# A state-space layer kernel: step-size columns moved into the token-major projection, decay tiles on VectorE one step ahead, row transposes one step later

## The chip, the cores and the metric

The kernel runs on one core of one Trainium2 chip. The metric is device microseconds of the whole program, from first to last instruction of one execution. Before the change it took 2696.54 us (median of 3 runs, 2694.78 to 2699.78).

## The reference, cut to what matters

Two layers over 1024 tokens of width 1024. Each layer mixes tokens in three ways (differential attention, dilated attention, a Mamba-2 state-space scan with 6 heads in chunks of 128 tokens) and then applies a gated MLP.

```python
proj = h @ w_in[layer]                       # 1024 x 3206 columns
dq, dk, dv, lq, lk, lv, z, xbc, dt = jnp.split(proj, IN_OFFSETS, axis=-1)
...
dt = jax.nn.softplus(dt + dt_bias)           # 6 columns: the step sizes
a = dt * A                                   # per head and token
Lmat = jnp.exp(segsum(a))                    # decay inside a chunk
xdt = x * dt_c[..., None]
y_diag = einsum('bclgn,bcsgn->bcgls', Cm, Bm) * Lmat @ xdt      # inside a chunk
y_off = Cm @ prev * jnp.exp(a_cs)            # from the chunks before
y = (y_diag + y_off + x * D) * jax.nn.silu(z)
out = grouped_rms_norm(y) * norm_gain        # two groups of 192 columns
...
mix = concatenate([o_diff, o_dil, o_ssd]) @ w_out[layer]
x = x + rms_norm(mix, post_mix_norm[layer])
```

## The kernel before

Every layer works on the tokens in two halves (T = 0 and 1, 512 tokens each). All projections are float32 products made of three fp32r matmuls: activations and weights are split into a high and a low part, and high x high, high x low and low x high are added in PSUM. `wsplit` (L130 to L134) loads a weight tile of 128x1024 (tile `wr`, 3 buffers, its DMA issued on SP's queue), copies it to `wh` on ScalarE (L133) and subtracts on VectorE to get `wl` (L134); `wh` and `wl` have 4 buffers each.

Most projections have the weights stationary and 512 tokens moving (`mm3`, L202, L205, L206). The columns that are needed token-major (dilated V, differential V, the gate z) come from `tm_in` through `tm_units` (L152, L155, L156): here 128 tokens are stationary and weight columns move. A *unit* is one block of columns for one tile of 128 tokens, 24 matmuls. `tm_in` has two blocks of 512 columns; each block takes four weight tiles, two of the eight row groups each, and four units, one for each token tile. So the next block's first weight tile can be split only when the last unit of the block before has gone past the buffer, and its fourth tile can be loaded only when the first one's split has given a `wr` buffer back. The evacuation (L772 to L777) copies the columns out, applies the gate and stores them to DRAM tensor `VZ`.

The six step-size columns have their own path, `dt_unit(T)` (L425 to L466): 16 matmuls with 12 or 6 stationary columns and 512 moving tokens, 8 small selecting matmuls that turn the 12 rows into token-major columns (L436), a chain of small VectorE instructions on 128x24 tiles for softplus (L439 to L459), and four matmuls for the running sums (L464).

The scan is `ssd(T)` (L470 to L581), a generator with 14 steps for four chunks. The first step of a chunk loads its rows (`cxa` from CX, `cxz` from VZ), builds two decay tiles of 128x768 (L502: the high part on POOL, the low part on VectorE, tiles named P), transposes x (L506, `xdt`, L508 and L510), and multiplies the decay tiles by a triangle (L528, L529). The second step masks (L532), calls `finish` for the chunk before (L481 to L488: three transposes of its normalised rows `yq`, L483) and reads the carried state (L543). The third step is the product inside the chunk (L552), the new state (L558) and the grouped norm, which ends in two ScalarE copies that write `yq` (L575).

`weave(dense, mixer, counts)` sets the order: for each dense unit it lets `counts` steps of a mixer generator go in behind given matmuls of the unit. Three weaves follow each other in a layer: units of the second attention and the scan's inputs beside attention(0) and the two `dt_unit`s; units for half 1 and `tm_in(1)` beside the rest of attention(0) and ssd(0); and the first output units (`out_units(0)`) beside what is left. After the output units come the rest of `tm_in(1)`, with the normalisation of half 0 (`pre_a`, `pre_b`, `norm_add`, L236 to L270) in between (`follow`). Differential attention's output norm is deferred in two parts: `f1` (L665 to L677, a VectorE chain with one POOL instruction) and `f2` (four transposes, L682) two steps behind.

Of the kernel before, what the change touches and what calls it, by code (L numbers as in the profile page):

```python
# [19 lines left out]
NL = 2  # L20
# [43 lines left out]
K_ID, K_SEL, K_TRI, K_MD, K_ML = 0, 128, 148, 276, 276 + 640  # L64
# [5 lines left out]
def body(ctx, tc, x_in, win, wtm, wdt, wout, wup, wdn, cst, gains, dtb, alog, lamp, kst, rope, out):  # L70
# [15 lines left out]
    sel = kc[:, K_SEL:K_SEL + 8]  # L86
    mhalf = kc[:, K_SEL + 8:K_SEL + 16]
# [15 lines left out]
    def tiny(n=4):  # L103
        return ss.tile([P, 8], F32, tag="tiny", bufs=16, name="tiny")
# [23 lines left out]
    def wsplit(src, nk):  # L128
        raw = sp.tile([P, KT * P], F32, tag="wr", bufs=3, name="wr")
        Y.dma_start(raw[:, :nk * P].rearrange("p (a n) -> p a n", a=src.shape[1]) if len(src.shape) == 3 else raw[:, :nk * P], src)  # L130
        hi = sp.tile([P, KT * P], F32R, tag="wh", bufs=4, name="wh")
        lo = sp.tile([P, KT * P], F32R, tag="wl", bufs=4, name="wl")
        A.activation(hi[:, :nk * P], raw[:, :nk * P], AF.Copy)  # L133
        V.tensor_tensor(lo[:, :nk * P], raw[:, :nk * P], fr(hi[:, :nk * P]), op=ALU.subtract)  # L134
# [11 lines left out]
    def tm3(a, pair, tk, hi, lo, k0, nk, n0, n):  # L146
        for k in range(nk):
            kk = k0 + k
            w = slice(k * H, (k + 1) * H)
            xh, xl = pair[kk]  # L150
            xh, xl = xh[:, tk], xl[:, tk]
            i = T_.matmul(a[:], xh, hi[:, w], start=(n0 + k == 0), stop=False)  # L152
            if n0 + k == 0 and hold[0] is not None:
                queue_behind(i, hold[0])
            T_.matmul(a[:], xh, lo[:, w], start=False, stop=False)  # L155
            lastmm[0] = T_.matmul(a[:], xl, hi[:, w], start=False, stop=(n0 + k == n - 1))  # L156
        marks.append(lastmm[0])

    def tm_units(w, k0, nk, pair, evac, before=None, inner=False, pairs=0):

        def tiles(c):
            return [(i, min(2, nk - i)) + wsplit(w[c, :, k0 + i:k0 + min(i + 2, nk)], min(2, nk - i) * 4)
                    for i in range(0, nk, 2)]

        def unit(c, t, ts):
            a = acc()
            for i, n, hi, lo in ts:
                tm3(a, pair, slice(t * P, (t + 1) * P), hi, lo, i, n, i, nk)
            evac(c, t, a)

        if inner:
            ts = [tiles(c) for c in range(2)]
            for t in range(4):
                for c in range(2):
                    unit(c, t, ts[c])
                    yield
            return
        for c in range(2):
            ts = tiles(c)
            if c < pairs:  # L180
                for t in (0, 2):
                    aa = [acc(), acc()]
                    for i, n, hi, lo in ts:
                        for x in range(2):
                            tm3(aa[x], pair, slice((t + x) * P, (t + x + 1) * P), hi, lo, i, n, i, nk)
                        if i == 2:
# [109 lines left out]
    for l in range(NL):  # L296
        lam_init = 0.8 - 0.6 * math.exp(-0.3 * l)
        def layer_constants():
# [23 lines left out]
            wd = ss.tile([P, KT, 12], F32R, tag="wd", bufs=1, name="wd")  # L322
# [750 lines left out]
```

## Time and profile before

| | before |
|---|---|
| median of 3 runs | 2696.54 us (2694.78 to 2699.78) |
| the profiled execution, and its span | 2697.55 us, 2695.8 us |
| PE (TensorE matmul) busy | 2625.3 us, 97% |
| DVE (VectorE) busy | 1830.1 us, 68% |
| ACT (ScalarE) busy | 1246.8 us, 46% |
| POOL (GpSimd) busy | 252.4 us, 9% |

PE executes its instructions in order, and matmuls overlap: a 512-column matmul is drawn 0.39 us long but the next one starts 0.227 us later. So the cost of a matmul is read from start to start. An entry in brackets, such as `[2.11 <-POOL P L502]`, is idle time of that engine just before the instruction and what ended it. PEclk is the granted clock as a share of 2.4 GHz.

### The profile page before, as it was taken

The numbers are of one execution on the slowest core, as the hardware profiler recorded it, in microseconds if no ns is written. First come the engines' busy times: TensorE is split into PE (matmuls) and PEld (weight loads), VectorE is DVE, ScalarE is ACT, GpSimd is POOL, SyncE is SP. The second block draws the span as 40 slices with busy tenths as digits, with TensorE's granted clock in tenths as the row PEclk, the third lists the DMA queues.
The fourth block names the chain that finished last, engine by engine and source line by source line (L and its number), as shares of the span: only waits on it lengthen the run. The fifth ranks groups of instructions, "written<-read, shape, count | busy, mean of one in ns | idle before, by whom it ended". The sixth has DMA issues, their size and how long they took to land. (4 is left out here: it accounts for less than half of the span.)

```text
span 2695.8 us, 36379 instructions
## 1 busy us (share of the span) xinstructions
PE 2625.3 (97%) x13160; PEld 2135.6 (79%) x13160; DVE 1830.1 (68%) x3814; ACT 1246.8 (46%) x2167; POOL 252.4 (9%) x244
## 2 busy tenths in 40 slices
PE   7999999999999999999999999999999999999998
PEld 5887777888778877888888877778887888788886
DVE  5566767566877676666765677575678775956666
ACT  4463444555544444333444644455555344543333
POOL 0100220110002010000002002201100110100001
PEclk9999999999999999999999999999999999999999
DMA  6653546343333354233257536354344334633222
GB/s 226 215 175 111 187 150 186 108 129 114 99 123 124 117 185 156 94 97 99 85 182 228 160 107 204 118 187 114 106 125 134 99 117 125 229 97 101 94 95 70
DMA packets 157348, 368.82 MB, mean 137 GB/s; under 512 B 18032, under 2 KB 53744, under 8 KB 157168
## 3 DMA queue, kind: packets, MB, share of 16 engines
q1 hardware_dynamic: 157168, 366.49, 43.4%
q8 instruction: 104, 1.70, 0.3%
q14 instruction: 76, 0.62, 0.1%
HBM read 306.13 MB, written 60.29 MB: 136 GB/s over the span
## 5 line engine op out<-in xcount | busy, mean ns | idle before, releaser
L202 PE MATMUL acc<-ah,wh 128*128 128x512 f32 x1952 | 775.6, 398 | 0.5 <-ACT ah L253 0.5
L205 PE MATMUL acc<-al,wh 128*128 128x512 f32 x1952 | 764.5, 392 | 0.0
L206 PE MATMUL acc<-ah,wl 128*128 128x512 f32 x1952 | 763.6, 391 | 0.0
L134 DVE TENSOR_TENSOR wl<-wr,wh 128x1024 fp32r<-128x1024 f32 (+1 forms) x390 | 470.5, 1209 | 264.1 <-ACT wh L133 259.8
L133 ACT ACTIVATE wh<-wr 128x1024 fp32r<-128x1024 f32 (+1 forms) x390 | 403.9, 1040 | 432.9 <-PE acc L205 254.4
L202 PEld LDWEIGHTS acc<-ah,wh 128*128 128x128 f32 x1952 | 367.1, 188 | 81.6 <-issue 9.6
L206 PEld LDWEIGHTS acc<-ah,wl 128*128 128x128 f32 x1952 | 367.2, 188 | 77.5 <-issue 1.0
L205 PEld LDWEIGHTS acc<-al,wh 128*128 128x128 f32 x1952 | 367.5, 188 | 73.0 <-issue 1.2
L361 DVE SCALAR_TENSOR_TENSOR cv<-acc,cs,cv 128x511 f32<-128x511 f32 (+2 forms) x436 | 324.4, 744 | 12.2 <-ACT cv L359 10.3
L152 PE MATMUL acc<-wh,g 128*128 128x512 f32 x704 | 282.3, 401 | 7.7 <-DVE ustate L364 3.7
L155 PE MATMUL acc<-wl,g 128*128 128x512 f32 x704 | 277.2, 394 | 3.0 <-DVE wl L134 3.0
L156 PE MATMUL acc<-wh,g 128*128 128x512 f32 x704 | 275.1, 393 | 0.6 <-DVE g L820 0.6
L598 ACT ACTIVATE P<-P,tiny 128x128 f32<-128x128 f32 (+7 forms) x224 | 173.2, 774 | 146.8 <-DVE tiny L597 141.4
L595 DVE CUSTOM_DVE_ANT_0 P<-s,kc 128x512 f32<-128x512 f32 (+3 forms) x224 | 130.5, 588 | 122.2 <-PE s L593 115.8
L155 PE MATMUL acc<-wl,ah 128*128 128x512 f32 x512 | 204.8, 401 | 7.5 <-DVE wl L134 7.4
L152 PE MATMUL acc<-wh,ah 128*128 128x512 f32 x512 | 205.4, 404 | 4.3 <-ACT ah L253 2.4
L156 PE MATMUL acc<-wh,al 128*128 128x512 f32 x512 | 203.6, 400 | 2.8 <-DVE al L254 2.8
L115 POOL TENSOR_TENSOR rs_r<-rs_m,kc 128x1 f32<-128x1 f32 (+2 forms) x88 | 66.0, 754 | 1337.6 <-DVE rs L116 1326.8
L152 PEld LDWEIGHTS acc<-wh,g 128*128 128x128 f32 x704 | 132.9, 189 | 42.2 <-issue 7.1
L359 ACT ACTIVATE cv<-acc,cs 128x512 f32<-128x512 f32 x204 | 155.5, 762 | 9.2 <-PE acc L206 8.2
L840 DVE TENSOR_TENSOR fT<-acc,fT 128x512 f32<-128x512 f32 x160 | 108.7, 686 | 73.0 <-PE acc L156 72.5
L156 PEld LDWEIGHTS acc<-wh,g 128*128 128x128 f32 x704 | 132.7, 189 | 31.0 <-DVE g L820 3.4
(183 smaller groups left out, 3169.4 us busy)
## 6 DMA issues: line engine op xcount, KB each, us to landing
wr<-in_wup SPq DMA_DIRECT2D x176, 512.0 KB, 3.6
wr<-in_wdn SPq DMA_DIRECT2D x80, 512.0 KB, 3.6
wr<-in_win SPq DMA_DIRECT2D x54, 512.0 KB, 4.5
wr<-in_wtm SPq DMA_DIRECT2D x32, 512.0 KB, 5.3
wr<-in_wout SPq DMA_DIRECT2D x32, 512.0 KB, 4.3
xd<-t SPq DMA_DIRECT2D x24, 512.0 KB, 2.9
t<-xd SPq DMA_DIRECT2D x24, 512.0 KB, 3.7
t<-in_x SPq DMA_DIRECT2D x16, 512.0 KB, 4.8
```

The lines of the kernel that those rows point to most:

```text
L133: A.activation(hi[:, :nk * P], raw[:, :nk * P], AF.Copy)
L134: V.tensor_tensor(lo[:, :nk * P], raw[:, :nk * P], fr(hi[:, :nk * P]), op=ALU.subtract)
L152: i = T_.matmul(a[:], xh, hi[:, w], start=(n0 + k == 0), stop=False)
L155: T_.matmul(a[:], xh, lo[:, w], start=False, stop=False)
L156: lastmm[0] = T_.matmul(a[:], xl, hi[:, w], start=False, stop=(n0 + k == n - 1))
L202: i = T_.matmul(a[:], hi[:, w], xh, start=(k == 0), stop=False)
L205: T_.matmul(a[:], hi[:, w], xl, start=False, stop=False)
L206: i = T_.matmul(a[:], lo[:, w], xh, start=False, stop=(k == nk - 1))
L359: A.activation(u[:], a[:], AF.Identity, scale=w[:, n:n + 1], bias=w[:, taps:taps + 1])
L361: V.scalar_tensor_tensor(u[:, d:], a[:, :H - d], w[:, n - d:n - d + 1], u[:, d:], op0=ALU.mult, op1=ALU.add)
L595: V.tensor_tensor_reduce(p[:, c:c + n], s[:, :n], mask[:, o:o + n], 1.0, -1e30 if c == 0 else mx[:, e], ALU.add, ALU.max, mx[:, e])
L598: A.activation(p[:, :nk * P], p[:, :nk * P], AF.Exp, scale=scale, bias=nm[:, e], accum_out=den[:, e])
```

## The change

1. `tm_in` gets three blocks of columns instead of two: 384 (dilated V), 262 (differential V and the six step-size columns), 384 (gate). `wsplit` and `tm_units` take blocks of any width; the weight tensors are `wva`, `wvb`, `wvz`.
2. `dt_unit` goes. The step-size columns come out of the 262-column units already token-major and get their bias there; `dt_chain` (the VectorE chain) runs behind the last 262-column unit for half 0, and as the first part of `dt_steps(1)` after attention(1) for half 1.
3. In `ssd`, `prepare(c)` loads a chunk's rows and builds both decay tiles on VectorE, one step before the chunk's first step; `finish` moves behind the next `yield`. The generator has 16 steps instead of 14, and `f2` is deferred one step more.

```diff
-    def tm3(a, pair, tk, hi, lo, k0, nk, n0, n):
+    def tm3(a, pair, tk, hi, lo, k0, nk, n0, n, width=H, step=H):
+        a = a[:, :width]
...
-            w = slice(k * H, (k + 1) * H)
+            w = slice(k * step, k * step + width)
...
-        def dt_unit(T):
-            a = acc()
-            r = rhs_of(hT[T])
-            for k in range(KT):
-                T_.matmul(a[:12], wd[:, k, :], r[k][0], start=(k == 0), stop=False)
-                T_.matmul(a[:6], wd[:, k, 0:6], r[k][1], start=False, stop=(k == KT - 1))
-            yield
-            d = t2("cv", 4)
-            A.activation(d[:12], a[:12], AF.Copy)
-            p = tr()
-            for c in range(4):
-                T_.matmul(p[:, c * 6:c * 6 + 6], d[:12, c * P:(c + 1) * P], sel[:12, 0:6], start=(c == 0), stop=(c == 3))
-            yield
+        dtr = [ss.tile([P, 24], F32, tag=f"dtr{T}", bufs=1, name="dtr") for T in range(2)]
+
+        def dt_chain(T):
...
+        def dt_steps(T):
+            dt_chain(T)
+            yield
+            dt_sums(T)
             yield
...
-            todo = None
-            for c in range(4):
-                cxa = sp.tile([P, 8, P], F32, tag="K", bufs=4, name="cxa")
+            def prepare(c):
+                cx = sp.tile([P, 8, P], F32, tag="K", bufs=4, name="cxa")
                 cxz = t2("Q", 4)
...
-                for x, at, E in ((ahi[T][:, c * 6:c * 6 + 6], ath, G), (col(5, c), atl, V)):
-                    E.tensor_tensor(at[:, :768].rearrange("p (h s) -> p h s", h=6),
+                for x, at in ((ahi[T][:, c * 6:c * 6 + 6], ath), (col(5, c), atl)):
+                    V.tensor_tensor(at[:, :768].rearrange("p (h s) -> p h s", h=6),
                                     tri.unsqueeze(1).to_broadcast([P, 6, P]), b6(x, P), op=ALU.mult)
+                return cx, cxz, ath, atl
+
+            todo = None
+            ahead = prepare(0)
+            yield
+            for c in range(4):
+                cx, cxz, ath, atl = ahead
...
-                if todo:
-                    finish(*todo)
                 first = T == 0 and c == 0
...
                 yield
+                if todo:
+                    finish(*todo)
                 yd = tr()
...
                 todo = (c, yq)
+                if c < 3:
+                    ahead = prepare(c + 1)
                 yield
+            yield
             yield
             finish(*todo)
...
-                    defer(z + 3, f2)
+                    defer(z + 4, f2)
...
         def tm_in(T, before=None):
             def evac(c, t, a):
                 v = t2("cv", 4)
-                if c == 0:
-                    A.activation(v[:], a[:], AF.Copy)
+                c0, n = ((0, 384), (384, 256), (640, 384))[c]
+                v, a, d = v[:, :n], a[:, :n], a[:, n:n + 6]
+                if c < 2:
+                    A.activation(v, a, AF.Copy)
                 else:
-                    A.activation(v[:, P:], a[:, P:], AF.Tanh, scale=0.5)
-                    A.activation(v[:, :P], a[:, :P], AF.Copy)
-                    V.scalar_tensor_tensor(v[:, P:], v[:, P:], 1.0, a[:, P:], op0=ALU.add, op1=ALU.mult)
-                Y.dma_start(VZ[T][t, :, c * H:(c + 1) * H], v[:])
-            return tm_units(wtm[l], 0, KT, rhs_of(hT[T]), evac, before, pairs=0 if before else 1)
+                    A.activation(v, a, AF.Tanh, scale=0.5)
+                    V.scalar_tensor_tensor(v, v, 1.0, a, op0=ALU.add, op1=ALU.mult)
+                Y.dma_start(VZ[T][t, :, c0:c0 + n], v)
+                if c == 1:
+                    e = slice(t * 6, t * 6 + 6)
+                    V.tensor_tensor(dtr[T][:, e], d, sm[:, e], op=ALU.add)
+                    if t == 3 and T == 0:
+                        dt_chain(0)
+            return tm_units([wva[l], wvb[l], wvz[l]], 0, KT, rhs_of(hT[T]), evac, before, pairs=0 if before else 1)
...
+        dt_sums(0)
         run(units(DILC, (0,)))
-        mix0 = chain(attn(0, DILH), dt_unit(0), dt_unit(1), attn(0, DIFH))
+        mix0 = chain(attn(0, DILH), attn(0, DIFH))
...
-        mix1 = chain(attn(1, DILH + DIFH), ssd(1))
+        mix1 = chain(attn(1, DILH + DIFH), dt_steps(1), ssd(1))
```

The first place is TensorE at the second step of a chunk in ssd(0), layer 0: the transposes of the last chunk's rows `yq` (L483 before) beside the reads of the carried state (L543 before, L555 now). Before:

```order
L152 MATMUL acc<-wh,ah 128x512
L483 MATMUL tr<-kc,yq 128x128
L543 MATMUL tr<-prev,cxa 128x192
L483 MATMUL tr<-kc,yq 128x128 x2
L543 MATMUL tr<-prev,cxa 128x192
L155 MATMUL acc<-wl,ah 128x512
```

And now (L492 is the transpose of `yq`):

```order
L168 MATMUL acc<-wh,al 128x384
L555 MATMUL tr<-prev,cxa 128x192 x2
L164 MATMUL acc<-wh,ah 128x384
L167 MATMUL acc<-wl,ah 128x384
L168 MATMUL acc<-wh,al 128x384
```

The transposes of `yq` have left this place; they stand 12 matmuls of 384 columns behind it, ahead of the product inside the chunk.

The second place is SP's queue around the second halves' token-major blocks, layer 0, behind the output units (kh and kl are loads for attention(1), xd the stored residual rows, gb a gain, t a residual reload). Before:

```order
L130 DMA wr<-in_wtm 128x1024 x3
L275 DMA xd_3824<-t_3753 128x1024
L621 DMA kh<-LK 64x1024 x2
L275 DMA xd_3877<-t_3755 128x1024
L130 DMA wr<-in_wtm 128x1024
L621 DMA kl<-LK 64x1024 x2
L275 DMA xd_3930<-t_3757 128x1024
L130 DMA wr<-in_wup 128x1024 x3
```

And now:

```order
L143 DMA wr<-in_wvb 128x2x262
L143 DMA wr<-in_wvz 128x768 x2
L293 DMA xd_3983<-t_3810 128x1024
L143 DMA wr<-in_wvz 128x768
L795 DMA VZ_77<-cv 128x256
L638 DMA kh<-LK 64x1024 x2
L795 DMA VZ_77<-cv 128x256
L293 DMA xd_4036<-t_3812 128x1024
L795 DMA VZ_77<-cv 128x256
L251 DMA gb<-in_gains 128x1024
L638 DMA kl<-LK 64x1024 x2
L795 DMA VZ_77<-cv 128x256
```

Behind the last of these rows stands the fourth tile of the third block (`wvz`): it is issued only behind the stores of all four 262-column units and two key loads. Before, one fourth tile was loaded here; now there are two, one for each block switch.

The third place is VectorE in the third chunk of ssd(0), layer 0, from its transposed x (L508 before, L522 now) to its masking (L532 before, L546 now) and a little beyond. Before:

```order
L508 TENSOR_TENSOR xdt<-tr,dtv 128x384
L522 TENSOR_TENSOR Q<-tr,kc 128x256
L502 TENSOR_TENSOR P<-kc,dtv 128x768
L513 TENSOR_TENSOR y<-tr,sm 128x384
L114 TENSOR_SCALAR rs_m<-tiny 128x2
L116 TENSOR_SCALAR rs_3482<-tiny 128x2
L121 TENSOR_TENSOR rs_q<-rs_r 128x2
L122 TENSOR_TENSOR rs_q<-rs_q,rs_3482 128x2
L123 SCALAR_TENSOR_TENSOR rs_r<-rs_q,rs_r 128x2
L532 TENSOR_TENSOR P<-P,Q 128x768
```

And now:

```order
L522 TENSOR_TENSOR xdt<-tr,dtv 128x384
L527 TENSOR_TENSOR y<-tr,sm 128x384
L145 TENSOR_TENSOR wl<-wr,wh 128x1024
L536 TENSOR_TENSOR Q<-tr,kc 128x256
L509 TENSOR_TENSOR P<-kc,adt 128x768
L546 TENSOR_TENSOR P<-P,Q 128x768
L558 TENSOR_TENSOR ys<-tr,dtv 128x384
L509 TENSOR_TENSOR P<-kc,dtv 128x768
L145 TENSOR_TENSOR wl<-wr,wh 128x1024 x2
```

The decay tiles here (L509) are those of the fourth chunk: the high part, which POOL built before, stands ahead of the third chunk's masking, and the low part behind it. The norm's chain (L114 to L123 before) no longer stands between.

## Rows read from the trace of the kernel before

**Rows 1.** The page's busy times: engine, busy us (share of the span), instructions.

```profile
PE 2625.3 (97%) x13160; PEld 2135.6 (79%) x13160; DVE 1830.1 (68%) x3814; ACT 1246.8 (46%) x2167; POOL 252.4 (9%) x244
```

**Rows 2.** PE's waits: line and what it waited for, us in total, times, longest.

```profile
PE acc L155 <- DVE wl L134: 10.4, 6, 2.6
PE tr L483 <- ACT yq L575: 5.4, 6, 1.1
PE s L593 <- DVE tiny L595: 4.3, 6, 1.6
PE s L528 <- POOL P L502: 4.2, 2, 2.1
PE tr L682 <- DVE on L677: 4.1, 2, 2.1
```

**Rows 3.** PE's timeline at dt_unit: start, duration, engine, line, operation.

```profile
213.07 0.40 PE L429 MATMUL acc<-ah,wd 128*12 128x512 f32 x1
...
216.78 0.40 PE L205 MATMUL acc<-al,wh 128*128 128x512 f32 x1
...
227.91 0.40 PE L429 MATMUL acc<-ah,wd 128*12 128x512 f32 x1
...
233.26 0.39 PE L206 MATMUL acc<-ah,wl 128*128 128x512 f32 x1
...
245.06 1.05 PE L436 MATMUL tr<-kc,cv 12*128 12x6 f32 x8
```

**Rows 4.** PE's timeline, narrower matmuls: a pair of 256 columns, four of 384.

```profile
118.15 0.40 PE L593 MATMUL s<-k,Q 128*128 128x256 f32 x2
118.39 0.40 PE L206 MATMUL acc<-ah,wl 128*128 128x512 f32 x1
...
366.62 0.34 PE L528 MATMUL s<-P,gtr 128*128 128x384 f32 x1
...
367.33 0.39 PE L155 MATMUL acc<-wl,ah 128*128 128x512 f32 x1
```

**Rows 5.** The page's costliest groups: busy us, mean ns of one, idle before.

```profile
L134 DVE TENSOR_TENSOR wl<-wr,wh 128x1024 fp32r<-128x1024 f32 (+1 forms) x390 | 470.5, 1209 | 264.1 <-ACT wh L133 259.8
L202 PEld LDWEIGHTS acc<-ah,wh 128*128 128x128 f32 x1952 | 367.1, 188 | 81.6 <-issue 9.6
```

**Rows 6.** Line 502, the decay tiles: duration ns min/median/max, first and last start.

```profile
L502 POOL TENSOR_TENSOR P<-kc,adt x16: 1462/2230/2454, 318.6 to 2169.7; 128x768 fp32r<-128x768 f32 x16
L502 DVE TENSOR_TENSOR P<-kc,dtv x16: 947/1487/2274, 320.1 to 2170.7; 128x768 fp32r<-128x768 f32 x16
```

**Rows 7.** VectorE's timeline, the chain of f1 before the transposes of L682.

```profile
328.13 0.69 DVE L669 TENSOR_TENSOR on<-tr,tiny 128x512 f32<-128x512 f32 x1 [0.91 <-PE tr L665]
...
333.21 0.69 DVE L677 TENSOR_TENSOR on<-on,rs_r 128x512 f32<-128x512 f32 x1
```

**Rows 8.** Stretches: length, busy of PE, PEld, DVE, ACT, POOL (instructions), PEclk, DMA.

```profile
341.00:381.00 40.00, 35.81 (x196) 30.05 (x196) 29.35 (x53) 20.08 (x48) 15.41 (x14) 1.00 0.54 170
380.80:384.20 3.40, 3.40 (x10) 2.62 (x9) 1.60 (x5) 1.56 (x4) 0.00 (x0) 0.51 0.00 0
```

**Rows 9.** Timeline, fourth tile of the second block, half 0 of layer 0.

```profile
44.28 0.33 SPq L130 DMA_DIRECT2D wr<-in_wtm  x1
...
49.94 1.06 ACT L133 ACTIVATE wh<-wr 128x1024 fp32r<-128x1024 f32 x1 [2.78 <-DMA wr<-in_wtm]
...
51.04 0.73 PE L152 MATMUL acc<-wh,ah 128*128 128x512 f32 x2 [1.89 <-ACT wh L133]
```

**Rows 10.** Timeline, the same tile in half 1 of layer 0.

```profile
426.27 2.35 DVE L134 TENSOR_TENSOR wl<-wr,wh 128x1024 fp32r<-128x1024 f32 x2
...
427.54 0.50 PE L155 MATMUL acc<-wl,ah 128*128 128x512 f32 x1 [2.57 <-DVE wl L134]
```

**Rows 11.** The page's DMA issues: KB each, median us from issue to landing.

```profile
wr<-in_wup SPq DMA_DIRECT2D x176, 512.0 KB, 3.6
...
wr<-in_wtm SPq DMA_DIRECT2D x32, 512.0 KB, 5.3
```

More of the change, by code (lines that the diff above doesn't have):

```diff
@@ L69, in body @@
 @with_exitstack
-def body(ctx, tc, x_in, win, wtm, wdt, wout, wup, wdn, cst, gains, dtb, alog, lamp, kst, rope, out):
+def body(ctx, tc, x_in, win, wva, wvb, wvz, wout, wup, wdn, cst, gains, dtb, alog, lamp, kst, rope, out):
     nc = tc.nc
@@ L103, in tiny @@
     def tiny(n=4):
-        return ss.tile([P, 8], F32, tag="tiny", bufs=16, name="tiny")
+        return ss.tile([P, 8], F32, tag="tiny", bufs=22, name="tiny")
     def fr(ap):
@@ L177, in tm_units @@
             return
-        for c in range(2):
+        for c in range(nc_):
             ts = tiles(c)
@@ L182, in tm_units @@
                     aa = [acc(), acc()]
-                    for i, n, hi, lo in ts:
+                    for y in ts:
                         for x in range(2):
-                            tm3(aa[x], pair, slice((t + x) * P, (t + x + 1) * P), hi, lo, i, n, i, nk)
-                        if i == 2:
+                            part(aa[x], c, t + x, *y)
+                        if y[0] == 2:
                             yield
@@ L690, in attn @@
             load_head(its[0][0], 1, T)
-            for z in range(n + 2 + 3):
+            for z in range(n + 2 + 4):
                 for f in later.pop(z, []):
@@ L797, in evac @@
                     norm_add(4 * T + t, xs[t], rr[t][:], sq[t], rr[t], g1, False, g2)
-            return tm_units(wout[l], 0, KT, rhs_of(pair), evac, pairs=1 if T else 0), rr
+            return tm_units([wout[l, c] for c in range(2)], 0, KT, rhs_of(pair), evac, pairs=1 if T else 0), rr
         def up_pair(T, j, pair):
@@ L855, in evac @@
                     fin.append(fin_norm(4 * T + t, xs[t], f[t], g3, g0))
-            return tm_units(wdn[l], k0, n, [gt[k0 + k] for k in range(n)], evac, inner=last and T == 1)
+            return tm_units([wdn[l, c] for c in range(2)], k0, n, [gt[k0 + k] for k in range(n)], evac, inner=last and T == 1)
         fin = []
@@ L951, in body @@
         nu = 44 + 8 * (NG - 2)
-        ns = 45 + 14 + 4
+        ns = 46 + 2 + 17
         kinds = []
@@ L1025, in rows @@
         return a.reshape(NL, -1, 128, 2, 512).transpose(0, 3, 2, 1, 4)
-    o["wtm"] = rows(np.concatenate([w[:, :, 1536:1920], w[:, :, 512:768], w[:, :, 1920:2304]], 2))
-    o["wdt"] = w[:, :, 3200:3206].reshape(NL, 8, 128, 6).transpose(0, 2, 1, 3)
+    for n, a in (("wva", w[:, :, 1536:1920]), ("wvb", np.concatenate([w[:, :, 512:768], w[:, :, 3200:3206]], 2)),
+                 ("wvz", w[:, :, 1920:2304])):
+        o[n] = a.reshape(NL, 8, 128, -1).transpose(0, 2, 1, 3)
     o["wout"] = rows(f["w_out"])
@@ L1051, in layout @@
     return {n: np.ascontiguousarray(v) for n, v in o.items()}
-_INS = ["x", "win", "wtm", "wdt", "wout", "wup", "wdn", "cst", "gains", "dtb", "alog", "lamp", "kst", "rope"]
+_INS = ["x", "win", "wva", "wvb", "wvz", "wout", "wup", "wdn", "cst", "gains", "dtb", "alog", "lamp", "kst", "rope"]
 def kernel(**inputs):
```

78 lines of the change are left out of this document (42 added, 36 removed).

## The prediction, made blind

> **What bounds the kernel now.** I read the page's busy times first: PE is busy for 97% of the span, VectorE for 68% [rows 1]. So the time changes by what is taken from or added to TensorE's in-order stream, or by its waits. Then the list of PE's waits [rows 2], then the timelines around those that the change touches. Waits outside the change (the start, the MLP) stay.
>
> **Removed: the step-size matmuls.** In layer 0 the first 16 run from 213.07 to 216.78, 3.71 us; the second 16, with the first 8 selecting matmuls among them, from 227.91 to 233.26, 5.35 us; the last 8 selecting matmuls take 1.05 us [rows 3]. That is 10.1 us a layer, 20.1 in two. The four matmuls of the running sums stay.
>
> **Added columns.** The 262-column block has 6 columns more, in 24 matmuls for each of 4 token tiles, 2 halves and 2 layers: 384 matmuls x 6 columns. Four 384-column matmuls take 0.71 us, 0.46 ns a column [rows 4]: +1.1 us.
>
> **More, narrower matmuls.** Three blocks have 288 matmuls in a half where two had 192, 384 more in all, for the same columns. Sixteen 512-column matmuls took 3.71 us [rows 3], 0.232 each; two of 256 took 0.24, 0.12 each [rows 4], so two halves cost within 8 ns of a whole. I take 0; the bounds are 0 and 384 x 16 ns = +6 us (the 384-column pace as a straight line with the 512-column one leaves 16 ns for a matmul without columns).
>
> **f2 one step later.** TensorE waits 4.1 us in two places for the chain of f1 [rows 2]. The chain takes 5.8 us from its first to its last instruction (328.13 to 333.90) [rows 7]; 17 dense matmuls stood between f1's and f2's transposes, now 30 do (7.0 us at 0.232). The wait goes: -4.1 us. What is late next is nothing: the stored row is read only in the output projection.
>
> **ssd(0): decay tiles and row transposes.** The stretch 341 to 381 holds 40 us with 35.8 of PE [rows 8], so some 4 us of waits. Two kinds end: L528 on POOL's tile (4.2 us in two layers) and L483 on `yq` (5.4 us, 6 times) [rows 2]. Behind the long POOL wait the granted clock is 0.51 for 3.4 us [rows 8], the lower level (1.2 GHz), and the same work needs 1.7 us more; so with both layers 4.2 + 5.4 + 3.4 = 13.0 us is at stake. POOL's tile took 1.46 to 2.45 us; VectorE's own 0.95 to 2.27 [rows 6]. Two on VectorE, a step ahead, are no longer waited for. The `yq` chain keeps its parts: product inside the chunk, two sums, new state, norm, two copies. It gets 12 more 384-column matmuls (2.1 us) before TensorE needs it, but ssd(0) also runs beside narrower units now, so a step's dense cover shrinks by a quarter. I keep a wait of 1.2 us at one chunk and 2.2 at another, 3.4 a layer: 13.0 - 6.8 = -6.2 us (bounds 0 and -13).
>
> VectorE pays for the 16 tiles that leave POOL. The price is between the least and the mean on its line, 0.95 and about 1.6 us [rows 6]; I take 0.95, since the long ones lie beside POOL's tile, which is gone. That is 15 us of VectorE work where 29 of 40 us are busy now [rows 8]: hidden, unless it stands ahead of a weight split that TensorE needs (rival 2). The Trainium skill (SBUF — State Buffer, Who interferes with whom) says that VectorE reading two SBUF operands and a GpSimd instruction reading SBUF exclude each other for a whole instruction. The spread on that line fits it, and by it the tile costs 0.95 and its neighbours get shorter; by the mean of the line the sum would have 16 x 0.65 = 10 us more of VectorE work.
>
> **dt chain.** Its small VectorE instructions ran between those of the attention rows, and L593 waits 4.3 us for VectorE there, up to 1.6 at a time [rows 2]; I take a quarter of that as gone: -1.0 (0 to -4).
>
> Gains: -20.1 + 1.1 - 4.1 - 6.2 - 1.0 = **-30.3 us** (-20 to -36).
>
> **What the third block costs.** This is the part that speaks against the change. A block's fourth weight tile is loaded only when the first tile's split has freed a `wr` buffer, and that only when the last unit of the block before has passed its first six matmuls. Before, the half 0 case of layer 0: issue at 44.28, split started at 49.94 when the tile had landed (5.6 us), TensorE waited 1.89 us for it [rows 9]. With last-unit start T, 512 columns: T + 6 x 0.23 + split 1.06 and 1.21 [rows 5, 9] + 0.3 for handing over = T+3.9, + landing L + 1.06; needed at T + 24 x 0.23 + 18 x 0.23 = T+9.7. The wait is L - 4.7, 0.9 with L = 5.6; measured 1.9. The formula is not too high.
>
> For 262 to 384 columns: T + 6 x 0.12 + splits of three quarters (0.8 and 0.9) + 0.3 = T+2.7, + L + 0.8; needed at T + 24 x 0.12 + 18 x 0.178 = T+6.1. The wait is L - 2.6, and some 0.5 more for the low part. Landings are 3.6 (quiet) and 5.3 us (in this place) for 512 KB [rows 11]; a 384 KB tile at L = 4.3 gives 2.2, with bounds 0.5 and 3.2. The Trainium skill (DMA: Bandwidth & Descriptors, Anatomy of one DMA) fits a transfer as 2.0 us plus its bytes at 436 GB/s, an estimate of 2.9 us for 384 KB; the rows here (5.6 us for 512 KB, where the same fit gives 3.2) are far above it, and by its figure this wait would be under 1 us. It is this switch, one in each half and layer, that before did not have:
> - layer 0, half 0: the transposes of half 1 lie beside it and cover 1 us: +1.8 with the low part.
> - layer 1, half 0: +2.7.
> - half 1, twice: normalisation of half 0 shares VectorE here, as in the 2.57 us that TensorE waits for a split behind 2.35 us of splits [rows 10]. `wvz`'s fourth tile stands on SP's queue behind two key loads and four VZ stores, each waiting for its own evacuation, its third tile's split behind the normalisation: 2.4 + 1.1, and 0.8 for late transposes: +4.3 each, 8.6.
>
> The first switch (to 262 columns) changes too: 18 x 0.12 us instead of 18 x 0.23 until the fourth tile is needed, 2 us less, of which smaller splits give back 1. Layer 0 half 0: the tile is also issued behind a VZ store, +1.8; layer 1: +1.2; half 1: +1.3 each. Together +5.6.
>
> The lower clock stood behind a 2.11 us wait [rows 2, 8]; I price it at 1.7 us with an even chance or better behind new waits of that length: 1.7 + 1.0 + 0.9 x 2 = +4.5. The start of layer 0 needs three smaller tiles: -0.7.
>
> Losses: 1.8 + 2.7 + 8.6 + 5.6 + 4.5 - 0.7 = **+22.5 us** (8 to 34; with the narrow-matmul bound up to 38).
>
> **Sum.** -30.3 + 22.5 = -7.8 on the profiled execution's 2697.55 us (span 2695.8) gives 2689.8; that execution stands 1 us above the median of the runs. I forecast 2690 us.
>
> **Rivals.**
> 1. *The fourth tiles land in time* (L near 3.6, units between cover them). Losses fall to about 8: -22, 2675 us. For it: the quiet median of 3.6 us [rows 11]. Against it: the rows for this place have 5.3 and 5.6.
> 2. *VectorE becomes the bound in ssd(0) and at the half-1 switches* (slower side). Place: the stretch of [rows 8], 29 of 40 us busy, takes 7 to 12 us of decay tiles while its dense work shrinks by a quarter. Price: TensorE waits for splits queued behind decay tiles, 5 us a layer, with a stretch of lower clock, 1.7, = +13, to 2703 us. It decides once a tile costs 1.6 us rather than 0.95, or two stand ahead of a split. For it: the wait of L155 is already the longest in this list [rows 2]. Against: 11 us of slack before.
> 3. *The step-size matmuls were only filling time that VectorE needs*: the attention rows woven around them now wait instead, and about 12 of 19 us come back; 2690 + 8 to 12 = 2698 to 2702, no change. For it: L593's waits on VectorE in this place [rows 2]. Against: the rows of the step-size matmuls show no idle time before them [rows 3].
> 4. *Narrow matmuls bound by their weight loads*: +6 or more. The pair at 0.12 us, each with its own load [rows 4], speaks against; 2696.
>
> **Chances.** Forecast 0.53, rival 1 0.19, rival 2 0.13, rival 3 0.11, rival 4 0.04. About 0.2% (5.4 us) is what a measurement of this kernel tells from no change: below 2691 is faster, above 2702 slower. The forecast's own range, 2681 to 2698, is faster in six of ten cases: 0.32 + 0.19 + some of rival 3, 0.01 = 0.52 faster; 0.21 + 0.09 + 0.04 = 0.34 the same; 0.14 slower, rival 2 and a rest. The range 2675 to 2702 leaves out about one in ten at each end.
>
> **What would show it.** The rows of L429, L430, L436 are gone, and so are PE's waits on POOL's P and on `on`. Two 262-column matmuls start 0.12 us apart. New PE waits on `wl` or `wh` stand at the second switch, near 40 to 60, 440, 1395 and 1770 us, 2 to 3 us each, with a granted clock near 0.5 behind some. A decay tile takes about 0.95 us. Wrong if the waits at these switches sum to under 8 us (rival 1), or if waits on VectorE in ssd(0) grow (rival 2).

## The result, and the profile after

The changed kernel takes **2670.28 us** (median of 4 runs, 2669.15 to 2673.96) against 2697.87 of the kernel before in the same comparison: ratio 0.9899 [0.9886, 0.9911], 27.6 us less. The forecast was 2690 with a range down to 2675; the time lies below it. The profiled execution took 2669.15 us, its span is 2667.4 us.

The page's busy times after, beside [rows 1]:

```profile
PE 2605.3 (98%) x13448; PEld 2163.8 (81%) x13448; DVE 1832.6 (69%) x3854; ACT 1247.7 (47%) x2179; POOL 230.3 (9%) x228
```

PE's busy time fell by 20.0 us, so some 8 us of the gain come out of idle time. PE's waits after, beside [rows 2] (the lines have moved: L134, which makes `wl`, is now L145, L133, which makes `wh`, is L144, L483 is L492, L593 is L610):

```profile
PE tr L268 <- DVE P L259: 10.4, 4, 7.8
PE acc L167 <- DVE wl L145: 8.1, 12, 1.5
PE acc L164 <- ACT wh L144: 6.7, 6, 2.2
PE tr L492 <- ACT yq L589: 5.5, 6, 1.5
...
PE s L610 <- DVE tiny L612: 1.3, 2, 0.6
```

The waits on POOL's tile (4.2 us) and on `on` ahead of f2's transposes (4.1 us) have no row any more, and `tiny` fell from 4.3 to 1.3. Most of the first row is the start of the program, which was there before (7.8 us now, 8.0 before). The waits on split weights, `wl` and `wh`, are 14.8 us together; before, they were 10.4 [rows 2] and 1.9 (the one of [rows 9]), 12.3 us. The decay tiles, beside [rows 6] (duration in ns min/median/max):

```profile
L509 DVE TENSOR_TENSOR P<-kc,adt x16: 941/948/1012, 283.3 to 2153.6; 128x768 fp32r<-128x768 f32 x16
L509 DVE TENSOR_TENSOR P<-kc,dtv x16: 942/947/958, 284.1 to 2155.4; 128x768 fp32r<-128x768 f32 x16
```

Both take 0.95 us, with no spread. The next rows are stretches, beside [rows 8]:

```profile
330.10:333.50 3.40, 3.40 (x13) 3.40 (x12) 2.19 (x7) 1.17 (x5) 0.00 (x0) 0.50 0.40 132
300.00:320.00 20.00, 19.32 (x109) 17.17 (x108) 17.05 (x26) 8.80 (x17) 5.02 (x5) 1.00 0.66 217
320.00:340.00 20.00, 18.07 (x101) 17.00 (x100) 14.74 (x30) 9.04 (x24) 8.48 (x8) 0.91 0.50 152
```

The scan of half 0 now lies some 35 us earlier, so 300 to 340 is the stretch to hold against 341 to 381 before: PE is busy for 37.4 of 40 us there (35.8 before) and VectorE for 31.8 (29.4 before). Stretches of 3.4 us at a granted clock of 0.5 (1.2 GHz), such as the first row, stand behind some of TensorE's stalls (1.5 us on `yq` at 327; 2.1 and 0.7 us on a split at 406), not behind all: the same 2.1 and 0.7 us in layer 1, at 1727, have none. Counted up to the last matmul there are 5 after and 8 before; each loses half its length, 1.7 us.

**Where 28.6 us between the start of the span and the last matmul went** (summed over all of PE's rows of the two profiled executions): waits 59.3 to 50.7, -8.6; half clock 13.7 to 8.5, -5.1; what is left, -14.9, is work: the step-size matmuls -20.1, columns +1.1, and a remainder of +4.1, which stands for the narrower matmuls.

### The profile page after: what moved, and what is told of

Read it like the earlier page. It is cut to its first block, busy times and chain, and to the rows that moved or that the text cites. A ratio compares the mean times of both kernels' runs of the same rounds, so it can differ in the third digit from the quotient of the medians.

```text
span 2667.4 us, 37072 instructions
## 1 busy us (share of the span) xinstructions
PE 2605.3 (98%) x13448; PEld 2163.8 (81%) x13448; DVE 1832.6 (69%) x3854; ACT 1247.7 (47%) x2179; POOL 230.3 (9%) x228
## 4 chain that ended last, share of the span: by engine, by line
PE 81%; DVE 9%; ACT 3%; DMA 3%; issue 3%; POOL 1%; SPq 0%; ACTq 0%; DVEq 0%; POOLq 0%
PE acc L220 16%; PE acc L223 15%; PE acc L224 15%; PE acc L168 7%; PE acc L164 7%; PE acc L167 7%; PE po L760 4%; PE s L610 3%; PE tr L750 3%; DVE wl L145 1%; POOL rs_r L114 1%; ACT wh L144 1%; DVE P L287 1%; DVE t L288 1%; DMA cv<-MT 1%
## 5 line engine op out<-in xcount | busy, mean ns | idle before, releaser
L145 DVE TENSOR_TENSOR wl<-wr,wh 128x1024 fp32r<-128x1024 f32 (+3 forms) x406 | 477.9, 1183 | 274.9 <-ACT wh L144 271.1
L144 ACT ACTIVATE wh<-wr 128x1024 fp32r<-128x1024 f32 (+3 forms) x406 | 406.2, 1007 | 470.0 <-PE acc L223 269.1
L164 PE MATMUL acc<-wh,ah 128*128 128x512 f32 (+2 forms) x640 | 225.4, 356 | 10.0 <-ACT wh L144 6.7
L167 PE MATMUL acc<-wl,ah 128*128 128x512 f32 (+2 forms) x640 | 226.3, 354 | 5.8 <-DVE wl L145 5.1
L168 PE MATMUL acc<-wh,al 128*128 128x512 f32 (+2 forms) x640 | 225.1, 353 | 4.3 <-DVE al L272 4.1
L114 POOL TENSOR_TENSOR rs_r<-rs_m,kc 128x1 f32<-128x1 f32 (+2 forms) x88 | 71.4, 815 | 1398.4 <-DVE rs L115 1256.6
L167 PEld LDWEIGHTS acc<-wl,g 128*128 128x128 f32 x704 | 133.0, 189 | 29.6 <-DVE wl L145 3.8
```

Source lines behind the costliest of these rows:

```text
L144: A.activation(h, r, AF.Copy)
L145: V.tensor_tensor(part(lo), r, fr(h), op=ALU.subtract)
L164: i = T_.matmul(a, xh, hi[:, w], start=(n0 + k == 0), stop=False)
L167: T_.matmul(a, xh, lo[:, w], start=False, stop=False)
L168: lastmm[0] = T_.matmul(a, xl, hi[:, w], start=False, stop=(n0 + k == n - 1))
```

## The experiments

Each ratio is to the kernel before in its own comparison.

**1. The three blocks and the step-size columns alone.** Scan, POOL's tile and f2 as before.

```diff
+            for c in range(4):
...
+                for x, at, E in ((ahi[T][:, c * 6:c * 6 + 6], ath, G), (col(5, c), atl, V)):
+                    E.tensor_tensor(at[:, :768].rearrange("p (h s) -> p h s", h=6),
...
-                    defer(z + 4, f2)
+                    defer(z + 3, f2)
```

> Three blocks and step sizes as moving columns, with the scan generator, the deferral of f2 and POOL's decay tile as before. Theory A (the change is two nearly independent gains; the third block costs its narrower matmuls, about 5 us, and hardly any wait): -20.1 us of step-size matmuls, +5.7 us of columns and narrower matmuls, -4 to -7 us of attention rows that no longer wait between the step-size instructions: -17 to -22 us against before, near 2678. Rival B (the waits near 260 us went with the scan's new steps, not with the step-size path): -9 to -14 us, near 2686, with L593's waits on VectorE still some 4 us.

Measured: 2698.09 us, 1.0004 [0.9995, 1.0012]. Nothing of the 20 us is left. Its waits:

```profile
PE tr L691 <- DVE on L686: 9.8, 2, 4.9
...
PE acc L164 <- DVE g L403: 3.8, 2, 1.9
...
PE tr L742 <- DVE P L727: 3.5, 2, 1.8
PE tr L742 <- DVE tiny L606: 3.3, 2, 1.7
```

They stand in the attention rows and the rope evacuations. The waits on splits are 14.8 us, as in the full change. All waits sum to 72 us and the half clock costs 18.8 us (11 stretches); the full change has 51 and 8.5. The longest new wait, for f2 (VectorE's chain of f1 is L678 to L686 here, L409 belongs to a rope evacuation):

```profile
291.37 0.68 DVE L678 TENSOR_TENSOR on<-tr,tiny 128x512 f32<-128x512 f32 x1
291.97 0.68 DVE L409 TENSOR_TENSOR g<-acc,g 128x512 f32<-128x512 f32 x1
...
298.98 1.22 DVE L120 TENSOR_TENSOR rs_q<-rs_r 128x8 f32<-128x8 f32 x1 [1.55 <-POOL rs_r L114]
...
302.69 1.09 PE L691 MATMUL tr<-kc,on 128*128 128x128 f32 x4 [4.90 <-DVE on L686]
```

The chain takes 11.2 us, 5.8 before [rows 7]. Three rope instructions and a weight split stand between its links, and three of its 128x8 instructions take 1.2 to 1.4 us (0.2 to 0.4 before), each beside an instruction of POOL.

**2. The scan and f2 alone**, on the kernel before. The new steps need places in a weave: first put into the first weave (`[3] * 4`), then at the end of the second.

```diff
-        weave(chain(units(DILC + DIFC, (1,)), tm1), mix0, [2] * 14)
+        weave(chain(units(DILC + DIFC, (1,)), tm1), mix0, [2] * 10 + [3] * 4)
```

> Before, with the scan's prepare step, both decay tiles on VectorE, the later row transposes and f2 one step later; step-size path and two blocks as before (four more steps of attention(0) go in beside the first four units, since the generators are longer). Theory A: f2's 4.1 us and the waits on POOL's tile of 4.2 us go, one stretch of lower clock with them in each layer (3.4 us), and the wait of the conv state copy beside ssd(1) (3.7 us, and one stretch of lower clock): -8 to -15 us, near 2687. Rival B (the scan's reordering carries most of the change): -18 us or more. Rival C (VectorE is the bound once it builds both tiles): 0 or slower.

> Before with the scan edit and f2 one step later alone, as e2_ssd_only, but with the four more steps behind (three instead of two in the last four units of the second weave), so that attention(0) stands where it stood. Expected of the scan edit by itself: the waits on POOL's tile (4.2 us) and for f2 (4.1 us) go, with two stretches of lower clock: -6 to -14 us, near 2687. If it is 0 again, the scan edit has no worth of its own without the step-size edit.

Measured: 2697.96 us, 1.0001 [0.9992, 1.0009], and 2681.88 us, 0.9935 [0.992, 0.995]. The first says more on where steps are put than on the scan: there f2 still waits 7.1 us. The second gives -16 us, more than the 6 to 14 expected: waits 49.3 us (59.3 before), half clock 3.4 (13.7). With experiment 1 (+0.8) the parts sum to -15; together they give -27.6. So some 12 us belong to neither part alone; but where the steps are put is by itself worth 16 us here, and the steps fall at other places in the full change, so the 12 us are not shown to come from the two parts alone.

**3. The third block alone**: 384, 256 and 384 columns on the kernel before, `dt_unit` kept.

```diff
-                Y.dma_start(VZ[T][t, :, c * H:(c + 1) * H], v[:])
+                Y.dma_start(VZ[T][t, :, c0:c0 + n], v)
+            return tm_units([wva[l], wvb[l], wvz[l]], 0, KT, rhs_of(hT[T]), evac, before, pairs=0 if before else 1)
```

> Before, with blocks of 384, 256 and 384 columns instead of two of 512, and nothing else: what the third block costs by itself. The prediction on record: +21 us (its losses without the six columns). Theory A: 384 more matmuls at 3 to 6 ns each beyond their columns, +4.6 us, and waits of 0 to 4 us at the first switch: +3 to +9 us, no wait over 1 us at the second switch.

Measured: 2714.13 us, 1.0058 [1.0046, 1.007], +16.8 us: waits +6.3, half clock +1.7, the rest, +8.7, work without a wait. The total is near the +21 of the prediction's losses, but it isn't made as they are: the waits on `wl` and `wh`, which were to be most of it, are 12.7 us against 12.3 before, and a half of it is in the matmuls, which had been put at nothing. The other theory, +3 to +9, is missed too.

**4. Is the second switch covered by the order?** The third block's units of half 1 in strict sequence.

```diff
+            if c >= strict:
+                hold[0] = lastmm[0]
...
+            return tm_units([wva[l], wvb[l], wvz[l]], 0, KT, rhs_of(hT[T]), evac, before, pairs=0 if before else 1, strict=2 if T else 9)
```

> The changed kernel with the units of the third block of half 1 strictly one behind the other on TensorE, where the changed kernel's order puts 42 matmuls of three units (on the first three weight tiles) ahead of the first one on the fourth tile, and the prediction reckoned with 18. Theory A (that order hides the fourth tile, which lands 4 to 5 us behind its issue there): +3 to +5 us in each layer, with a stretch of lower clock in one or both, together +6 to +13 us against the changed kernel, waits on wh or wl near 424 and 1744 us. Rival D (the tile lands soon enough by itself): under +2 us.

Measured: 2686.32 us, 0.9958 [0.9946, 0.997], 16 us above the full change (6 to 13 had been expected): waits +7.2, half clock +8.5. TensorE at the second switch of half 1, layer 0, with the strict sequence:

```profile
421.32 0.44 PE L167 MATMUL acc<-wl,ah 128*128 128x384 f32 x1 [0.42 <-DVE wl L145]
...
425.26 0.47 PE L164 MATMUL acc<-wh,ah 128*128 128x384 f32 x1 [2.80 <-ACT wh L144]
426.25 0.69 PE L167 MATMUL acc<-wl,ah 128*128 128x384 f32 x1 [0.52 <-DVE wl L145]
```

These 3.7 us (3.8 in layer 1) are near the 4.3 that the prediction took for this place. In the full change the tile is issued no earlier (0.9 us behind the block's first matmul in both; SP at 420.10) and lands at 425.2; its high part runs on ScalarE here:

```profile
425.28 0.85 ACT L144 ACTIVATE wh<-wr 128x768 fp32r<-128x768 f32 x1 [5.12 <-DMA wr<-in_wvz]
```

and yet TensorE has no wait of 0.2 us or more here: it has 42 matmuls of three units on the first three tiles ahead of the first one on the fourth. At 0.173 us that is 7.3 us, where the formula of the prediction had 18 (3.2 us).

**5. Fewer tiles at the first switch**: the 262-column block in three tiles (three, three and two row groups) instead of four; then the same with the row transposes one step earlier.

```diff
+            s = group[c] if group else 2
+            return [(i, min(s, nk - i)) + wsplit(w[c][:, k0 + i:k0 + min(i + s, nk)], widths[c])
+                    for i in range(0, nk, s)]
```

> The changed kernel with the 262-column block loaded as three weight tiles (3, 3 and 2 row groups) instead of four, so that it needs no fourth tile behind the first one's split. If the waits on wl and wh at the first switch (2.1 and 0.7 us at 406 and 1727 us, 1.3 us at 1368, 0.8 us at 47) are the fourth tile's: they go, with the lower clock behind them, -5 to -10 us against the changed kernel, near 2663. If they are the crowded VectorE and ScalarE queues beside the normalisation: under -3 us.

> The changed kernel with the two undone or added pieces that were no slower or a little faster by themselves: three weight tiles for the 262-column block, and the row transposes in the second step again. If they add up: 2 to 5 us under the changed kernel, near 2666; if the normalisation's wait that took the fourth tile's place is the bound: the same as with three tiles alone (2667.6).

Measured: 2667.58 us, 0.9893 [0.9878, 0.9908], and 2665.79 us, 0.9877 [0.9862, 0.9891]. With three tiles the splits of half 1 are no longer waited for at this switch, but the transposes of the normalised rows are, in the same place (the first of the two versions):

```profile
400.68 1.25 PE L269 MATMUL tr<-kc,P 128*128 128x128 f32 x8 [1.12 <-DVE al L273]
408.74 1.06 PE L269 MATMUL tr<-kc,P 128*128 128x128 f32 x8 [2.06 <-DVE P L260]
```

VectorE's normalisation sets the end here, the weight tile only stood in front of it. The second has the lowest median of the study, but the intervals of both versions overlap with that of the full change.

**6. Single parts taken out of the full change.** f2 one step earlier; the high tile on POOL, still a step ahead; the row transposes back in the second step; no look-ahead (both tiles on VectorE in the chunk's own step); no empty first step for half 0.

```diff
-                    defer(z + 4, f2)
+                    defer(z + 3, f2)
```

> The changed kernel with f2 two steps behind f1 as before, everything else as changed. Theory P: f1's chain takes 5.8 us and has some 15 to 20 dense matmuls for cover: a wait of 2 to 3 us in each layer, with a stretch of lower clock: +4 to +9 us against the changed kernel. Theory Q: +4 us at most, the wait alone.

```diff
+                for x, at, E in ((ahi[T][:, c * 6:c * 6 + 6], ath, G), (col(5, c), atl, V)):
+                    E.tensor_tensor(at[:, :768].rearrange("p (h s) -> p h s", h=6),
```

> The changed kernel with the high decay tile on POOL again, still one step ahead. Theory P: what counts is that the tile is built a step ahead; on POOL it is there in time too, and VectorE has 7.6 us less to do in each layer: within 4 us of the changed kernel. Theory Q (POOL's 1.5 to 2.4 us tiles hold up VectorE's instructions and the norms' pow behind them): +8 us or more, with longer VectorE instructions beside POOL and waits on yq of over 2 us.

```diff
+                if todo:
+                    finish(*todo)
...
-                if todo:
-                    finish(*todo)
```

> The changed kernel with the row transposes back in the second step of a chunk, as before; tiles on VectorE and a step ahead as changed. Both theories: the waits on yq grow by the 12 matmuls of 384 columns that lay between, up to 2 us at each of 4 to 6 places, where the list has 5.5 us now: +4 to +12 us against the changed kernel, with lower clock behind the longest.

```diff
-            ahead = prepare(0)
...
-                cx, cxz, ath, atl = ahead
+                cx, cxz, ath, atl = prepare(c)
```

> The changed kernel, all steps in their places (the scan's empty first step too), but a chunk's rows loaded and its two decay tiles built (on VectorE) in the chunk's first step itself instead of one step ahead. Theory S (what the scan edit brings is where its steps fall, one slot later beside f1's chain): within 4 us of the changed kernel. Theory L (the look-ahead itself): TensorE waits for decay tiles or loads at L542 in most chunks, +8 to +20 us against the changed kernel.

```diff
-            yield
+            if T:
+                yield
```

> The changed kernel without the yield behind prepare(0) in half 0: the scan of half 0 starts one slot earlier, so that its first step lies beside f1's VectorE chain again; look-ahead, VectorE tiles, late transposes and f2 as changed. Theory S: f1's chain is stretched from 5.8 to some 10 us, TensorE waits 2 to 4 us for f2 in each layer with lower clock behind: +6 to +14 us against the changed kernel. Theory L: under +3 us.

Measured, in this order: 2673.38 us, 0.9908 [0.9892, 0.9925] (f2's wait is back, 3.6 us in two places); 2672.23, 0.9904 [0.9889, 0.9919]; 2669.89, 0.9893 [0.9878, 0.9907]; 2676.15, 0.9927 [0.9911, 0.9944]; 2672.31, 0.9909 [0.9894, 0.9924]. Only the look-ahead can be told from the full change, by some 6 us. Taken singly the parts are worth 3 + 2 + 0 + 6 + 2 us: no sum of them makes 28. The row transposes had been expected at 4 to 12 us and are worth nothing that shows.

The profiles make these numbers sharper. These programs and that of the full change have the same first 1001 matmuls on TensorE; the last of them starts between 198.2 and 202.1 us, later where a stretch of half clock falls near 32 us, which no edit has touched. From there to the end of the span the full change takes 2469.2 us, these five 2472.7, 2468.6, 2470.7, 2475.5 and 2469.1. So by one profile each, f2's step is worth 3.5 us, the look-ahead 6.3, and the others at most 1.5.

**7. Where the 28 us sit.** From experiment 1 on: f2 one step later; then, beside it, an empty first step in half 0; or both tiles on VectorE in the old step.

```diff
-                    defer(z + 3, f2)
+                    defer(z + 4, f2)
```

> The three blocks and moving step-size columns (which alone gained nothing: 2698.1 against 2697.3 us) with one thing more: f2 one step later and attention one step longer. The scan and POOL's tile are as before. Theory P (the step-size matmuls' 20 us came back as waits because attention(0) and f1/f2 now run earlier, among the rope instructions of the units, and f2's distance and phase decide): the 9.8 us of waits at L691 go, and most of the lower clock behind them: -10 to -18 us against the three blocks alone, near 2683. Theory Q (the scan's tiles on POOL make VectorE and POOL late): the waits only change place, 0 to -6 us.

```diff
+            if T == 0:
+                yield
```

> Three blocks, moving step-size columns, f2 one step later (2693.9 us in the run before), the scan as in the old kernel with POOL's tile in the chunk's first step, and one empty step in front of the scan of half 0. Theory S: the 8.4 us of waits for f2 and most of the lower clock behind them go: -8 to -16 us against that kernel, near 2682. Theory L: -3 us at most.

```diff
-                for x, at, E in ((ahi[T][:, c * 6:c * 6 + 6], ath, G), (col(5, c), atl, V)):
+                for x, at, E in ((ahi[T][:, c * 6:c * 6 + 6], ath, V), (col(5, c), atl, V)):
```

> Three blocks, moving step-size columns, f2 one step later, the old scan (2693.9 us), and of the scan edit only this: the high decay tile on VectorE, still in the chunk's first step. Theory M: the rope products are no longer held up, VectorE does not wait for the rope table (2.7 us before), f2's waits of 8.4 us go for the most part: -8 to -16 us, near 2682. Theory N: within 4 us.

Measured: 2693.95 us, 0.9988 [0.9978, 0.9997]; 2703.43, 1.0018 [1.0006, 1.0031]; 2688.57, 0.9965 [0.9951, 0.9979]. A step more for f2 does not end its wait (8.4 us in two places, 9.8 before it); the theory that the scan only had to start a step later falls; the tile on VectorE gives 5 us, fewer than expected (f2's wait falls to 3.4, but `yq` keeps 9.7 and a wait of 4.7 on P comes).

**8. Both causes at once.** The full change with the high tile on POOL *and* without look-ahead.

```diff
+                for x, at, E in ((ahi[T][:, c * 6:c * 6 + 6], ath, G), (col(5, c), atl, V)):
...
-            ahead = prepare(0)
...
+                cx, cxz, ath, atl = prepare(c)
```

> The changed kernel with both halves of the tile edit undone at once: rows loaded and tiles built in the chunk's own first step, and the high tile on POOL; late transposes, f2 and the step counts as changed. One alone cost 2 us (POOL, a step ahead) and 6 us (VectorE, in the step). Theory M (POOL's tile in the step holds up the rope products on POOL, their stores on SP and the rope table behind them, and VectorE and TensorE wait): 15 to 25 us above the changed kernel, waits for f2 of some 4 us. Theory N (the costs add up): 6 to 10 us above it.

Measured: 2693.51 us, 0.9981 [0.9971, 0.9991]: 23 us lost, where the two edits alone lose 2 and 6 (behind the 1001st matmul 20.4, where they lose -0.6 and 6.3). Its timeline at the scan's first chunk in layer 0 (POOL, SP, VectorE and TensorE; L417 makes the low part of a rope row, L426 stores high and low parts, L364 loads a rope table, L402 begins the next rope evacuation, L683 to L691 is the chain of f1, L696 f2's transposes):

```profile
290.24 1.47 POOL L509 TENSOR_TENSOR P<-kc,adt 128x768 fp32r<-128x768 f32 x1 [5.84 <-ACT P L612]
294.05 4.78 POOL L417 TENSOR_TENSOR g<-g 128x512 fp32r<-128x512 f32 x2 [2.35 <-ACT g L415]
...
293.94 5.44 SPq L426 DMA_DIRECT2D MX<-g  x4
299.44 0.58 SPq L364 DMA_DIRECT2D g<-in_rope  x1
...
300.09 0.69 DVE L687 TENSOR_TENSOR cv<-on 128x512 f32<-128x512 f32 x1
303.58 0.69 DVE L402 TENSOR_TENSOR g<-acc,g 128x512 f32<-128x512 f32 x1 [2.80 <-DMA g<-in_rope]
304.19 0.68 DVE L689 TENSOR_REDUCE tiny<-cv 128x8 f32<-128x512 f32 x1
...
309.47 0.68 DVE L691 TENSOR_TENSOR on<-on,rs_r 128x512 f32<-128x512 f32 x1
...
310.30 0.63 PE L696 MATMUL tr<-kc,on 128*128 128x128 f32 x4 [4.35 <-DVE on L691]
```

And the full change in the same place (f1's chain is L686 to L694):

```profile
284.13 0.95 DVE L509 TENSOR_TENSOR P<-kc,dtv 128x768 fp32r<-128x768 f32 x1
...
289.61 1.27 POOL L417 TENSOR_TENSOR g<-g 128x512 fp32r<-128x512 f32 x1 [13.07 <-ACT g L415]
291.50 1.29 POOL L417 TENSOR_TENSOR g<-g 128x512 fp32r<-128x512 f32 x1 [0.62 <-ACT g L415]
...
290.76 2.57 SPq L426 DMA_DIRECT2D MX<-g  x4
293.67 0.53 SPq L364 DMA_DIRECT2D g<-in_rope  x1
...
297.38 0.69 DVE L694 TENSOR_TENSOR on<-on,rs_r 128x512 f32<-128x512 f32 x1
298.14 0.69 DVE L402 TENSOR_TENSOR g<-acc,g 128x512 f32<-128x512 f32 x1
...
298.51 0.60 PE L699 MATMUL tr<-kc,on 128*128 128x128 f32 x4
```

TensorE is 3.7 us later in the first from about 40 us on, so 3.7 us come off its times before they are held against the other's. Read it from the top: the two low parts on POOL take 4.78 us in one go (2.56 in the other), after 2.35 us in which POOL has nothing, so it isn't the tile ahead of them on POOL that holds them; they begin 0.7 us later and end 2.3 later, in company of VectorE's splits. The four stores, two of which need them, hold SP for 5.44 us (2.57); the rope table behind them is asked for at 299.44 (293.67), 2.1 us later; VectorE has the next rope evacuation (L402) in the middle of f1's chain and waits 2.80 us for that table, with the rest of the chain behind it; TensorE waits 4.35 us for the chain. Where both tiles are on VectorE in the chunk's own step (no look-ahead, above), the order on VectorE is another, the chain ahead of the evacuation, and TensorE's wait is the shorter one, though it has 17 matmuls between the transposes of f1 and of f2 here and 29 there:

```profile
300.68 0.69 DVE L691 TENSOR_TENSOR on<-on,rs_r 128x512 f32<-128x512 f32 x1
301.48 0.69 DVE L402 TENSOR_TENSOR g<-acc,g 128x512 f32<-128x512 f32 x1
...
301.52 0.63 PE L696 MATMUL tr<-kc,on 128*128 128x128 f32 x4 [1.68 <-DVE on L691]
```

So between these programs the order on TensorE, SP and VectorE differs as well as the tile's engine, and the runs don't separate the two.

The length of this chain of f1 (the second of half 0 in layer 0) divides the programs: 10.4 to 11.2 us in the old scan of experiment 1, in the first placing of experiment 2, in the first two programs of experiment 7 and in this one; 5.4 to 6.3 in the kernel before, the second placing of experiment 2, the full change, each of its versions in experiment 6, and the last of experiment 7. In the two pairs in which only the tile's engine was edited in the chunk's own step (POOL or VectorE) it goes from 10.8 to 5.4.

## Why the prediction was wrong

**The sum against the ledger.** By kind, the prediction's terms make -19.0 us of work, +10.1 of waits (18.7 at the weight switches, less 4.1 for f2, 2.8 in the scan, 1.0 for the step sizes and 0.7 at the start) and +1.1 of half clock: -7.8. The traces show -14.9, -8.6 and -5.1: -28.6. So of 20.8 us missed, 18.7 are waits and 6.2 half clock, and 4.1 of work go the other way.

**The step that failed: "What the third block costs", +22.5 us.** Its waits at the switches were put at 18.7 us; the waits on splits grew by 2.5. Its half clock was put at +4.5; the half clock fell by 5.1 in all, though single stretches come and go between profiles. The second switch (13.1 us) has no wait over 0.2 us anywhere: in half 1 the written order has 42 matmuls as cover, not 18, and without it 16 us come back (experiment 4); in half 0 the tile landed in 3.4 and 3.2 us, not 4.3. The prediction's estimate of 2.9 us lies nearer to these, but the fit behind it is given by the Trainium skill (DMA: Bandwidth & Descriptors, Anatomy of one DMA) for transfers issued from GpSimd; these tiles go by SP's queue, and in half 1 one took 5.1 us. The order stood in the program before it ran, so this could have been counted. At the first switch half 1 was right (0.35 + 0.50 + 2.10 + 0.74 = 3.7 us, taken at 3.9; the 0.35 ended with an instruction of the norm) and layer 1, half 0, nearly (1.5, taken at 1.2); layer 0, half 0, fell from 1.89 to 0.79 us where 1.8 more were taken.

This is what rival 1 said, with its sign (under 8 us at the second switch) and 2675 us. Its two reasons held in one half each: a landing near 3.6 us in half 0, cover by the units between in half 1.

**Removed matmuls: right.** They and the columns are -19 us of work; no idle time came in their own place. Narrow matmuls at nothing were wrong: +4.1 us, within the bound of 6. That the time nevertheless did not fall in experiment 1 is rival 3's outcome, but by another way than its wait on small VectorE instructions at L593.

**Parts 1 and 2 by themselves came out near by luck.** With what they cost they were put at -20.1 + 1.1 - 1.0 + 22.5 = +2.5 us, and experiment 1 gave +0.8. But its waits on splits are those of the full change; what fills the gap is 10 us of other waits, for f2's chain and in the attention rows, and 5 us of half clock, which the sum did not have.

**The second step that failed: "f2 one step later" and "ssd(0): decay tiles and row transposes", priced at -10.3 us by the waits of the kernel before.** They were worth 16 us in that kernel (experiment 2) and 28 on top of the parts 1 and 2 (2698.09 to 2670.28). In the kernel before, f1's chain [rows 7] has no other VectorE instruction between its links and takes 5.8 us; in experiment 1 rope instructions lie in it and POOL's beside it, and it takes 11.2. That the missing step-size steps brought them together is inferred from the order of the steps. The old scan costs TensorE more waits there (72 us against 51) and more half clock (18.8 against 8.5). The new scan escapes that in two ways, and one is nearly enough: the tile off POOL (6 us lost without the look-ahead) or a step ahead (none that shows lost on POOL); without both some 20 us are lost (experiment 8). So a wait that was not in the trace of before was paid for by parts 1 and 2 and taken away by part 3.

**Of the steps in that term** the waits on POOL's tile and on `on` went as foreseen, and a tile takes 0.95 us as taken. The later place of the row transposes, counted as 2.1 us of cover, is worth nothing that shows (experiment 6). The Trainium skill (SBUF — State Buffer, Who interferes with whom) had been weighed for the spread on that line: with POOL's tile gone the spread is gone (941 to 1012 ns), and with POOL's tile back beside it, in experiment 8, VectorE's tile takes up to 2.2 us. The trace agrees with the rule; what it doesn't tell is how far such a delay goes. `yq` kept 5.5 us of waits (6.8 taken). Rival 2 fell by its sign: VectorE is busier in the scan (31.8 of 40 us), yet TensorE waits there for it only 0.7 us on the mask and 0.3 on a split in layer 0, and under 0.3 at any other place. 3.7 us of waits on the convolution's state in the MLP went too, which the prediction had not looked at; they are gone in experiments 1 and 2 and there in 3, and no run tells why.

**Open.** Experiment 8 shows the loss with its price and its way at one place, not what of it is the tile on POOL and what the order that comes with it, nor what makes the 12 us by which the parts together exceed their sum; the tile alone on VectorE in experiment 7 halved f1's chain and gave 5 us where 8 to 16 were expected, so the empty first step, the later transposes and the tile act together in a way that these runs don't split.

## What to carry to other kernels

For a wait at a switch of weights, count the matmuls that the written order really puts ahead of the first one on the late tile. Price each part of a change in the order that the other parts leave behind, not in the trace of before. Before times of two profiles are held against each other, take off what they already differ by ahead of the change. And follow a late instruction on a little-used engine through the queues that work in order: the store that waits for it, the load behind that store, and the engine that waits for the load.

## What the runs showed of the hardware

A matmul's pace doesn't shrink quite with its columns: 0.227 us for 512, 0.173 for 384 (proportional: 0.170), 0.122 for 262 (0.116); these are medians from start to start. The first two rows have 384 columns, the last two 262:

```profile
424.03 0.33 PE L164 MATMUL acc<-wh,ah 128*128 128x384 f32 x1
424.21 0.33 PE L167 MATMUL acc<-wl,ah 128*128 128x384 f32 x1
...
399.05 0.28 PE L167 MATMUL acc<-wl,ah 128*128 128x262 f32 x1
399.17 0.28 PE L168 MATMUL acc<-wh,al 128*128 128x262 f32 x1
```

3 ns in 768 matmuls and 6 in 384 make 4.6 us, near the +4.1 of the ledger.

A small VectorE instruction can take several times as long beside POOL: in experiment 1 three of 128x8 elements took 1.2 to 1.4 us, each while POOL had a 128x512 or 128x768 instruction, and others of their kind 0.16 and 0.17 us.
